# Second norm's rows of a hybrid decoder layer: transposed by VectorE blocks and DRAM, or by TensorE

## Chip, core and metric

The kernel runs on one core of a Trainium2 chip. The metric is the device time of one execution in microseconds; lower is better. Before the change three runs took 954.28, 956.22 and 958.12 us, median 956.22. PE is TensorE, DVE VectorE, ACT ScalarE, POOL GpSimd, and SP is the engine whose queue issues most DMAs.

## The reference

One decoder layer on 1024 tokens and 16 learned meta tokens of width 1024, in float32. The part that matters here is its second half:

```python
mix = jnp.concatenate([attn, rec], axis=-1) @ w_out[l]
h = h + rmsnorm(mix, g_post_mix[l])
u = rmsnorm(h, g_pre_ffn[l])
f = jnp.square(jax.nn.relu(u @ w_ff1[l])) @ w_ff2[l]
h = h + rmsnorm(f, g_post_ffn[l])
```

`rmsnorm(x, g)` multiplies each row by `rsqrt(mean(x*x) + 1e-6)` and by `g`. `mix` has 1024 columns, `w_ff1` is 1024 x 4096.

## The kernel before

Every product of float32 operands is made from three matmuls on a high and a low part of each operand (`mm3`, L125, L130, L131); `split` makes the parts, the high one on ScalarE (L96), the low one on VectorE (L99).

The output projection works on eight tiles of 128 tokens. `out_mm(t, ...)` fills two PSUM banks of 512 columns with `mix` for tile t: for t from 0 to 3 most of it beforehand, for t from 4 to 7 all 48 matmuls in the loop over t. `out_norm(t, ...)` then loads the rows of x (L939, on SP), squares the banks on ScalarE (L944), raises the mean to the power -0.5 on GpSimd (`rstd_of`, L170 to L176), scales the banks on VectorE (L950), adds x (L953), stores the sum h to the output (L954, on SP; the last stage reads or accumulates on it), squares h on ScalarE (L956), and multiplies h by its own scale on VectorE (L958). The result is u without its weight g_pre_ffn, with tokens in partitions.

The next product needs u with its 1024 columns in partitions. `u2_tiles(t, xn)` does this: eight TensorE transposes of 128x128 into PSUM (L970), evicted with the multiplication by g_pre_ffn as a column per partition, four on ScalarE (L981), two double ones on VectorE (L975). They land in `u2f[half]`, four buffers of 128x2x512 for the tokens 0 to 511 (half 0) and four for 512 to 1023 (half 1). In the loop over t, tiles 0 and 1 are transposed at t = 4, tiles 2 and 3 at t = 5, tile 4 at t = 6, tiles 5 and 6 at t = 7, and tile 7 after the loop.

The product with `w_ff1` is a scheme of seven block products for a 2x2 split (Strassen's kind). Four products of the first blocks (`p1`, `p2` for p = 0 and 1, 12 matmuls each) and two more `p1` need half 0 alone (`b11`, `b21` are its splits). Then `t_sums` adds and subtracts both halves (L996), the sums are split into `ot2`, and the long loop over sixteen column blocks begins (`prep_a` loads and combines the weights, L993 and L996; `product`). `p2` adds its result on VectorE (L1110).

The order of instructions on each engine is made by a scheduler when the program is built, and each engine executes its own in that order. SP's queue is one such row: a DMA that waits holds up all DMAs behind it. Buffers come from tagged rings: "d" has four buffers (x rows among others), "raw" two (h and raw weights), "ws" five, "c" eight.

Of the kernel before, what the change touches and what calls it, by code (L numbers as in the profile page):

```python
# [9 lines left out]
F32 = mybir.dt.float32  # L10
F32R = mybir.dt.float32r
AF = mybir.ActivationFunctionType
ALU = mybir.AluOpType
# [3 lines left out]
P = 128  # L17
D = 1024
KC = D // P
# [18 lines left out]
def hybrid_layer(  # L38
# [6 lines left out]
    nc = tc.nc  # L45
# [7 lines left out]
    dpool = ctx.enter_context(tc.tile_pool(name="dpool", bufs=1, space=DRAM))  # L53
# [4 lines left out]
    def slot(tag, shape, dt=F32):  # L58
        uid[0] += 1
        return slab.tile(shape, dt, tag=tag, name=f"{tag}{uid[0]}", bufs=bufs[tag])  # L60

    def pair(tag, shape):
        return slot(tag, shape, F32R), slot(tag, shape, F32R)
# [255 lines left out]
    def normed(b):  # L319
        if b == 0:  # L320
            return [
                (norm_rows(meta_t[:NMETA], NMETA), NMETA),
                (norm_first(xt[0], True), P), (norm_first(xt[1], False), P),
            ]
        rows = [(xt[2 * b], P), (xt[2 * b + 1], P)]
        return [(norm_rows(s[:m], m), m) for s, m in rows]
# [65 lines left out]
    xn = normed(0)  # L392
# [105 lines left out]
    for b in range(4):  # L498
# [3 lines left out]
        if b == 0:  # L502

            acc = [bank("acc"), bank("acc")]
# [3 lines left out]
            xn = [(norm_rows(xt[2], P, True), P)]  # L508
# [7 lines left out]
            for w, (t0, n), sink, tag in (  # L516
                (wq, (16, 256), sink_q0, "o"), (wx, piece, sink_x0, "acc"),
            ):
                acc = bank(tag)
# [10 lines left out]
    for h in range(2):  # L530
        r, o, m = HALF[h], HALF[1 - h], slice(P - NMETA, 2 * P)
# [62 lines left out]
    for b in range(2):  # L594
        pv = bank("pt", (P, 4, P))
        for i in range(4):
            o = NMETA + (4 * b + i) * P
# [288 lines left out]
    for cs in ((0, 1), (2, 3)):  # L886
# [13 lines left out]
        for c in cs:  # L900
            for half in range(2):
                y = ys[c][:, 512 * half : 512 * half + 512]
# [14 lines left out]
    t4_dram = dpool.tile([P, 2, 4, 512], F32, name="t4_dram")  # L917

    u2f = [[None] * 4 for _ in range(2)]

    def out_mm(t, po, kcs):
        half, o = t // 4, (t % 4) * P
# [8 lines left out]
                )  # L931

    def out_banks(t):
        tag = ("pt", "o", "acc", "s", "pt", "acc", "s", "pt")[t]
        return [bank(tag), bank(tag)]

    def out_norm(t, po):
        xr = slot("d", [P, D])
        nc.sync.dma_start(xr, x[t * P : (t + 1) * P, :])  # L939
        h = slot("raw", [P, D])  # L940
        ssq = [small.tile([P, 1], F32, name=f"sq{n}", tag=f"sq{n}") for n in range(2)]
        for n in range(2):
            c = slice(512 * n, 512 * n + 512)
            nc.scalar.activation(  # L944
                h[:, c], po[n], AF.Square, scale=RMS_SC, accum_out=ssq[n]
            )
        rs = rstd_of(ssq)
        for n in range(2):
            c = slice(512 * n, 512 * n + 512)
            nc.vector.scalar_tensor_tensor(  # L950
                h[:, c], po[n], rs, gmix_b[:, c], op0=ALU.mult, op1=ALU.mult
            )
        nc.vector.tensor_tensor(h, h, xr, op=ALU.add)  # L953
        nc.sync.dma_start(out[t * P : (t + 1) * P, :], h)  # L954
        ssq2 = small.tile([P, 1], F32, name="ssq", tag="ssq")
        nc.scalar.activation(xr, h, AF.Square, scale=RMS_SC, accum_out=ssq2)  # L956
        rs2 = rstd_of([ssq2])
        nc.vector.tensor_scalar(xr, h, rs2, None, op0=ALU.mult)  # L958
        return xr

    def u2_tiles(t, xn):
        half = t // 4
        if u2f[half][0] is None:
            u2f[half] = [slot("c", [P, 2, 512]) for _ in range(4)]
        o = (t % 4) * P
        for k4 in range(0, KC, 4):
            pt = bank("o", (P, 4, P))
            for i in range(4):
                kc = k4 + i
                nc.tensor.transpose(pt[:, i, :], xn[:, kc * P : (kc + 1) * P], ident)  # L970
            for i in range(0, 4, 2):
                kc = k4 + i
                dst = u2f[half][kc // 2]
                if k4:
                    nc.vector.tensor_tensor(  # L975
                        dst[:, :, o : o + P], pt[:, i : i + 2, :],
                        g_ffn_col[:, kc : kc + 2].to_broadcast([P, 2, P]), op=ALU.mult,
                    )
                    continue
                for n in range(2):  # L980
                    nc.scalar.activation(  # L981
                        dst[:, n, o : o + P], pt[:, i + n, :], AF.Copy,
                        scale=g_ffn_col[:, kc + n : kc + n + 1],
                    )
# [113 lines left out]
    xns = {}  # L1098
# [13 lines left out]
    for t in range(8):  # L1112
        po = pos[t] if t < 4 else out_banks(t)
        out_mm(t, po, range(6 if t < 4 else 0, KC))
        for t_ in {4: (0,), 5: (2,), 6: (4,), 7: (5,)}.get(t, ()):
            u2_tiles(t_, xns[t_])
        xns[t] = out_norm(t, po)
        for t_ in {4: (1,), 5: (3,), 7: (6,)}.get(t, ()):
            u2_tiles(t_, xns[t_])
        if t == 4:  # L1120
            a11_early.update(early(0, 0, pair("a", ESH)))
        if t == 5:
            b11 = operand(u2f[0][0:2])
            a12_early.update(early(1, 0, pair("ws", ESH)))
        if t == 6:
            b21 = operand(u2f[0][2:4])
            hl = slot("b", ESH, F32R), slot("e", ESH, F32R)
            a11_early.update(early(0, 2, hl))
# [380 lines left out]
```

## Time and profile before

| | us |
|---|---|
| median of three runs | 956.22 (954.28 to 958.12) |
| span of the profiled execution | 955.3 |
| PE busy in the span | 943.8 (99%) |
| DVE busy | 655.7 (69%) |
| ACT busy | 505.9 (53%) |
| POOL busy | 129.1 (14%) |

For the profiled execution the profile lists its span alone. A row of a timeline has start, duration, engine, line, operation, output and inputs, and in brackets the idle time before it with what ended it. In the chain of waits each row is a piece of the chain that ended last: start, length, and what ran. A row of windows lists, for a stretch of time, the busy time of PE, PEld (weight loads), DVE, ACT and POOL with their counts, then the TensorE clock that was granted, the DMA engines' busy share and GB/s. Matmuls overlap, so the distance between two starts is what one costs, not its length.

### The profile page before, as it was taken

Reading aid. Unit: us, or ns where it says so; the run is one execution under the profiler, and the core shown is the slowest. Engines: PE = TensorE matmul, PEld = TensorE weight load, DVE = VectorE, ACT = ScalarE, POOL = GpSimd, SP = SyncE. Lnnn points to the kernel's source line nnn. Section 1 sums busy time; section 2 is a strip of 40 time slices with the busy share of each in tenths; the row PEclk is TensorE's granted clock in tenths of the full one; section 3 lists DMA queues with packets and bytes.
Section 4 is the critical chain, followed back from the end, with each engine's and each line's share of the span. In section 5 each row is a group of like instructions: output and inputs, shape, how many; then the busy total and the mean of one; then the engine's idle time right before and its main releaser. Section 6 shows DMA issues by size and latency. Waiting matters only on the chain.

```text
span 955.3 us, 12432 instructions
## 1 busy us (share of the span) xinstructions
PE 943.8 (99%) x4728; PEld 789.7 (83%) x4728; DVE 655.7 (69%) x845; ACT 505.9 (53%) x854; POOL 129.1 (14%) x189
## 2 busy tenths in 40 slices
PE   9999999999999999999999999999999999999996
PEld 8999999877888878888888888888887788888885
DVE  6567987788856787665644465476667576779893
ACT  7537766568645554444655575654433343446441
POOL 4102563520021100010000000001121100001201
PEclk9999999999999999999999999999999999999999
DMA  8221010204226368674422364334777765647934
GB/s 271 56 67 23 24 45 24 67 23 131 83 109 185 133 220 264 198 253 144 155 89 88 111 203 127 104 113 114 175 180 186 185 199 177 192 139 196 246 65 89
DMA packets 88199, 130.21 MB, mean 136 GB/s; under 512 B 13702, under 2 KB 52630, under 8 KB 88140
## 3 DMA queue, kind: packets, MB, share of 16 engines
q1 hardware_dynamic: 78972, 104.44, 34.0%
q0 software_dynamic: 8880, 24.19, 12.2%
q8 instruction: 37, 0.61, 0.3%
q10 hardware_dynamic: 288, 0.79, 0.2%
q14 instruction: 22, 0.18, 0.1%
HBM read 109.93 MB, written 18.87 MB: 135 GB/s over the span
## 4 chain that ended last, share of the span: by engine, by line
PE 88%; DVE 5%; ACT 3%; DMA 2%; POOL 1%; issue 1%; SPq 0%; DVEq 0%; ACTq 0%; POOLq 0%
PE ps_acc L130 10%; PE ps_acc L131 10%; PE ps_acc L125 10%; PE ps_s L131 6%; PE ps_s L130 6%; PE ps_s L125 6%; PE ps_pt L130 6%; PE ps_pt L131 6%; PE ps_pt L125 6%; PE ps_o L130 5%; PE ps_o L131 5%; PE ps_o L125 5%; ACT c L82 1%; PE ps_o L691 1%; PE ps_acc L282 1%
## 5 line engine op out<-in xcount | busy, mean ns | idle before, releaser
L99 DVE TENSOR_TENSOR ws<-raw,ws 128x1024 fp32r<-128x1024 f32 (+1 forms) x69 | 82.6, 1197 | 76.1 <-ACT ws L96 24.3
L96 ACT CAST ws<-raw 128x1024 fp32r<-128x1024 f32 (+1 forms) x68 | 69.7, 1026 | 87.9 <-PE ps_o L130 23.9
L96 ACT CAST ws<-e 128x1024 fp32r<-128x1024 f32 x41 | 43.0, 1049 | 82.8 <-PE ps_o L130 35.3
L125 PE MATMUL ps_acc<-a,ws 128*128 128x256 f32 (+2 forms) x256 | 85.8, 335 | 0.0
L130 PE MATMUL ps_acc<-a,ws 128*128 128x256 f32 (+2 forms) x256 | 85.5, 334 | 0.0
L131 PE MATMUL ps_acc<-a,ws 128*128 128x256 f32 (+2 forms) x256 | 85.0, 333 | 0.0
L99 DVE TENSOR_TENSOR b<-b,b 128x1024 fp32r<-128x1024 f32 (+2 forms) x50 | 58.9, 1177 | 24.8 <-PE ps_o L130 19.1
L96 ACT CAST b<-b 128x1024 fp32r<-128x1024 f32 (+2 forms) x49 | 49.9, 1019 | 46.4 <-DVE b L996 41.0
L99 DVE TENSOR_TENSOR ws<-e,ws 128x1024 fp32r<-128x1024 f32 x41 | 50.1, 1223 | 32.4 <-ACT ws L96 18.9
L680 POOL TENSOR_SCALAR_AFFINE_SELECT c<-c 128x512 fp32r<-128x512 f32 x64 | 53.6, 858 | 67.6 <-ACT c L96 59.3
L125 PEld LDWEIGHTS ps_acc<-a,ws 128*128 128x128 f32 x256 | 48.3, 189 | 4.7 <-issue 0.2
L131 PEld LDWEIGHTS ps_acc<-a,ws 128*128 128x128 f32 x256 | 48.3, 189 | 4.5
L130 PEld LDWEIGHTS ps_acc<-a,ws 128*128 128x128 f32 x256 | 48.2, 188 | 4.4 <-issue 0.4
L125 PE MATMUL ps_acc<-ws,b 128*128 128x512 f32 (+1 forms) x120 | 46.3, 387 | 1.1 <-ACT ws L96 1.1
L130 PE MATMUL ps_acc<-ws,b 128*128 128x512 f32 (+1 forms) x120 | 46.3, 386 | 0.5 <-DVE ws L99 0.4
L131 PE MATMUL ps_acc<-ws,b 128*128 128x512 f32 (+1 forms) x120 | 46.1, 385 | 0.0
L125 PE MATMUL ps_pt<-ws,b 128*128 128x512 f32 x112 | 44.4, 396 | 0.0
L130 PE MATMUL ps_pt<-ws,b 128*128 128x512 f32 x112 | 44.1, 394 | 0.0
L131 PE MATMUL ps_pt<-ws,b 128*128 128x512 f32 x112 | 44.0, 393 | 0.0
L125 PE MATMUL ps_s<-ws,b 128*128 128x512 f32 x110 | 43.4, 395 | 0.0
L131 PE MATMUL ps_s<-ws,b 128*128 128x512 f32 x110 | 43.3, 394 | 0.0
L130 PE MATMUL ps_s<-ws,b 128*128 128x512 f32 x110 | 43.3, 393 | 0.0
(416 smaller groups left out, 2662.0 us busy)
## 6 DMA issues: line engine op xcount, KB each, us to landing
raw<-in_w_ff_dram SPq DMA_DIRECT2D x61, 512.0 KB, 4.1
e<-in_w_ff_dram SPq DMA_DIRECT2D x45, 512.0 KB, 4.0
a<-in_w_ff_dram SPq DMA_DIRECT2D x12, 512.0 KB, 6.6
s_dram<-a POOLq DMA_DIRECT2D x12, 512.0 KB, 3.7
c<-in_x_dram SPq DMA_DIRECT2D x8, 512.0 KB, 4.0
raw<-in_w_in_dram SPq DMA_DIRECT2D x8, 512.0 KB, 3.7
d<-in_x_dram SPq DMA_DIRECT2D x8, 512.0 KB, 3.3
out_dram<-raw SPq DMA_DIRECT2D x8, 512.0 KB
```

The lines of the kernel that those rows point to most:

```text
L82: ins = nc.scalar.activation(*args, **kwargs).ins
L96: nc.scalar.copy(hi, src)
L99: low = nc.vector.tensor_tensor(lo, src, f32(hi), op=ALU.subtract).ins
L125: ins = nc.tensor.matmul(dst, lh, rh, start=start, stop=False, skip_group_check=True).ins
L130: nc.tensor.matmul(dst, lh, rl, start=False, stop=False, skip_group_check=True)
L131: last_mm[0] = nc.tensor.matmul(dst, ll, rh, start=False, stop=stop, skip_group_check=True).ins.name
L282: last_mm[0] = nc.tensor.matmul(acc[:, :n], w[k // 2][:, kc, :], u[kc][k % 2][:, t0 : t0 + n], start=k == 0 and kc == 0, stop=k == last an ...
L680: nc.gpsimd.affine_select(out=p_[:, :, s], in_=f32(p_[:, :, 0]), pattern=[[0, 4], [g, P]], compare_op=op, fill=0.0, base=0, channel_multip ...
L691: nc.tensor.matmul(po[:, oc : oc + n], v, p_[:, pc : pc + n], start=first and k == 0, stop=last and k == 1, skip_group_check=True,)
```

## The change

For tiles 0 to 6 the TensorE transposes and their evictions go. The weight g_pre_ffn is loaded as a row for all partitions (`gpre_b`, by a DMA on ScalarE's queue, into a "ws" buffer), and VectorE multiplies h by its scale and by this row at once. `by_blocks` then turns the tile: one VectorE instruction transposes all 32x32 blocks into a second "d" buffer, and four DMAs, one for each 32 partitions, write it to a DRAM scratch of 512 KB a tile in runs of 1 KB. `u2_read`, called one tile later, fetches the eight 128x128 pieces from there into the same `u2f` buffers, each in one DMA of 512 runs of 128 B. All twelve DMAs are on SP's queue. Tile 7 keeps the old way, and its projection takes the banks "o" instead of "pt".

```diff
@@ -917,6 +917,10 @@
     t4_dram = dpool.tile([P, 2, 4, 512], F32, name="t4_dram")
 
     u2f = [[None] * 4 for _ in range(2)]
+    LAST_BY_DMA = 6
+    u2_dram = dpool.tile([LAST_BY_DMA + 1, 4, P, 2 * P], F32, name="u2_dram")
+    gpre_b = slot("ws", [P, D])
+    nc.scalar.dma_start(gpre_b, g_pre_ffn[0].partition_broadcast(P))
 
     def out_mm(t, po, kcs):
         half, o = t // 4, (t % 4) * P
@@ -931,7 +935,7 @@
                 )
 
     def out_banks(t):
-        tag = ("pt", "o", "acc", "s", "pt", "acc", "s", "pt")[t]
+        tag = ("pt", "o", "acc", "s", "pt", "acc", "s", "o")[t]
         return [bank(tag), bank(tag)]
 
     def out_norm(t, po):
@@ -955,8 +959,33 @@
         ssq2 = small.tile([P, 1], F32, name="ssq", tag="ssq")
         nc.scalar.activation(xr, h, AF.Square, scale=RMS_SC, accum_out=ssq2)
         rs2 = rstd_of([ssq2])
-        nc.vector.tensor_scalar(xr, h, rs2, None, op0=ALU.mult)
-        return xr
+        if t > LAST_BY_DMA:
+            nc.vector.tensor_scalar(xr, h, rs2, None, op0=ALU.mult)
+            return xr
+        nc.vector.scalar_tensor_tensor(
+            xr, h, rs2, gpre_b, op0=ALU.mult, op1=ALU.mult
+        )
+        return by_blocks(xr, u2_dram[t])
+
+    def by_blocks(xn, dram, tag="d"):
+        y = slot(tag, [P, 4, KC, 32])
+        nc.vector.transpose(y, xn.rearrange("p (k b d) -> p b k d", k=KC, b=4))
+        for a in range(4):
+            nc.sync.dma_start(
+                dram[a].rearrange("(b d) r -> d b r", b=4),
+                y[32 * a : 32 * a + 32].rearrange("p b k t -> p b (k t)"),
+            )
+        return dram
+
+    def u2_read(t, dram):
+        half, o = t // 4, (t % 4) * P
+        if u2f[half][0] is None:
+            u2f[half] = [slot("c", [P, 2, 512]) for _ in range(4)]
+        for kc in range(KC):
+            nc.sync.dma_start(
+                u2f[half][kc // 2][:, kc % 2, o : o + P].rearrange("p (a t) -> p a t", a=4),
+                dram[:, :, 32 * kc : 32 * kc + 32].rearrange("a p t -> p a t"),
+            )
 
     def u2_tiles(t, xn):
         half = t // 4
@@ -1112,11 +1141,9 @@
     for t in range(8):
         po = pos[t] if t < 4 else out_banks(t)
         out_mm(t, po, range(6 if t < 4 else 0, KC))
-        for t_ in {4: (0,), 5: (2,), 6: (4,), 7: (5,)}.get(t, ()):
-            u2_tiles(t_, xns[t_])
         xns[t] = out_norm(t, po)
-        for t_ in {4: (1,), 5: (3,), 7: (6,)}.get(t, ()):
-            u2_tiles(t_, xns[t_])
+        if t:
+            u2_read(t - 1, xns[t - 1])
         if t == 4:
             a11_early.update(early(0, 0, pair("a", ESH)))
         if t == 5:
```

## The prediction

> **What bounds the kernel now.** I read the page first (span, engine totals), then the chain of waits around the stage that the change touches, then the windows and timelines of that stage.
>
> ```profile
> span 955.3 us, 12432 instructions
> ...
> PE 943.8 (99%) x4728; PEld 789.7 (83%) x4728; DVE 655.7 (69%) x845; ACT 505.9 (53%) x854; POOL 129.1 (14%) x189
> ```
>
> TensorE is busy for 99% of the span, so whatever leaves its queue should leave the time, unless a wait takes its place. The chain shows how near such a wait is (start us, us, what):
>
> ```profile
> 325.58 0.99 POOL rs L176
> ...
> 326.59 0.26 DVE d L958
> ...
> 330.68 0.60 DVE d L1110
> ...
> 334.82 0.66 DVE c L975 x2
> ...
> 349.89 0.60 DVE d L996
> ...
> 351.15 0.50 PE ps_acc L131
> ```
>
> ```profile
> 326.00:337.00 11.00, 11.00 (x58) 9.16 (x56) 10.54 (x18) 7.62 (x15) 1.20 (x2) 1.00 0.50 146
> 337.00:348.00 11.00, 11.00 (x49) 8.98 (x48) 10.20 (x17) 6.13 (x11) 0.00 (x0) 1.00 0.71 239
> ```
>
> The chain leaves TensorE for the scale of the last token tile (rs, ready at 326.57), runs for 24.6 us through VectorE, and releases TensorE at 351.15. VectorE (fourth figure of a window) is busy 10.54 and 10.20 of 11 us there. TensorE lost next to nothing yet, but there is no slack: if rs of tile 7 comes later, or if TensorE gets there sooner, TensorE waits.
>
> **What leaves TensorE.** Tile 4's 48 matmuls run from the first to the second of these starts, and the chain gives eight transposes 0.87 us:
>
> ```profile
> 270.89 0.40 PE L125 MATMUL ps_pt<-ws,b 128*128 128x512 f32 x1
> 281.96 1.03 PE L970 MATMUL ps_o<-ident,d 128*128 128x128 f32 x8
> ```
> ```profile
> 282.12 0.87 PE ps_o L970 x8
> ```
>
> A matmul costs 11.07/48 = 0.231 us. Seven tiles' transposes are 7 x 0.87 = 6.1 us. That is the whole possible gain. Their evictions on ScalarE and VectorE go too; of those only the pair of tile 6 (0.66, row above) lay on the chain.
>
> **What comes in, per tile.** One VectorE block transpose of 128x1024, a multiplication by two operands for a cheaper one by a scalar, four 128 KB writes and eight 64 KB reads on SP's queue. Rows:
>
> ```profile
> 226.95 2.31 DVE L851 TENSOR_TENSOR_SCAN c<-b,c 128x1040 f32<-128x1040 f32 x1
> 229.19 1.20 DVE L99 TENSOR_TENSOR a<-raw,a 128x1024 fp32r<-128x1024 f32 x1
> 265.83 1.23 DVE L953 TENSOR_TENSOR raw<-raw,d 128x1024 f32<-128x1024 f32 x1
> 269.25 0.76 DVE L958 TENSOR_SCALAR d<-raw,rs 128x1024 f32<-128x1024 f32 x1 [2.12 <-POOL rs L176]
> 270.07 1.41 DVE L950 SCALAR_TENSOR_TENSOR raw<-ps_o,rs,e 128x512 f32<-128x512 f32 x2
> ```
> ```profile
> L208 SPq DMA_DIRECT2D raw<-in_w_in_dram x13: 368/368/817, 23.0 to 170.8; - x13
> ```
> ```profile
> L939 SPq DMA_DIRECT2D d<-in_x_dram x8: 328/337/454, 237.8 to 303.7; - x8
> ...
> DMA to landing us min/median/max: 3.3/3.3/3.3
> ```
> ```profile
> 186.37 0.59 SPq L867 DMA_DIRECT2D raw<-in_w_out_dram  x1
> ```
> ```profile
> 267.08 0.35 SPq L954 DMA_DIRECT2D out_dram<-raw  x1
> ```
> ```profile
> 270.38 0.60 ACT L944 ACTIVATE raw<-ps_acc 128x512 f32<-128x512 f32 x1 [2.13 <-DMA out_dram<-raw]
> ```
> ```profile
> e<-in_w_in_dram SPq DMA_DIRECT2D x2, 256.0 KB, 5.0
> ...
> ws<-ws POOLq DMA_DIRECT2D x2, 36.0 KB, 2.0
> ```
>
> - Transpose: not in this trace. Between 0.76 (one input, a scalar) and 2.31 (the scan); I take 1.2, the usual pass over such a tile. The multiplication: 1.2, like L953.
> - Writes: issue 0.35 to 0.59 (32 of 128 rows; L867 has 64 and takes 0.59), I take 0.45. Landing 2.0 (the 36 KB copy) to 3.3 (the 512 KB store issued at 267.08 released ScalarE at 270.38); I take 2.5. So 3 x 0.45 + 2.5 = 3.85.
> - Reads: 0.37 each to issue (L208, also many short runs; up to 0.59), 8 x 0.37 = 3.0.
> - Load of x: 3.3 alone, up to 5.0 (slowest 256 KB load above).
>
> The reads are 4096 runs of 128 B a tile. The nearest rows are two loads of w_q at 81 us (2 x 1024 runs of 256 B) and one of 1024 runs of 512 B at 121 us; the last two figures are DMA share and GB/s:
>
> ```profile
> 82.00:83.00 1.00, 1.00 (x11) 1.00 (x10) 0.84 (x3) 0.98 (x5) 0.00 (x0) 1.00 0.70 162
> 83.00:84.00 1.00, 1.00 (x11) 1.00 (x10) 0.97 (x3) 0.90 (x3) 0.31 (x1) 1.00 1.26 285
> 84.00:85.00 1.00, 1.00 (x11) 1.00 (x11) 1.00 (x3) 0.00 (x0) 0.42 (x2) 1.00 0.43 94
> ...
> 122.00:123.00 1.00, 1.00 (x11) 1.00 (x10) 1.00 (x2) 0.08 (x1) 0.82 (x4) 1.00 0.42 104
> 123.00:124.00 1.00, 1.00 (x11) 1.00 (x10) 0.97 (x3) 0.00 (x0) 1.00 (x3) 1.00 1.12 339
> 124.00:125.00 1.00, 1.00 (x11) 1.00 (x10) 0.97 (x3) 0.86 (x3) 1.00 (x2) 1.00 0.27 81
> ```
>
> A 256 B run costs 2.39 x 16 / 2048 = 18.7 ns of an engine, a 512 B run 1.81 x 16 / 1024 = 28.3 ns; a line through both gives 14 ns at 128 B. I take 16: 256 runs per engine are 4.1 us a tile, 1.1 us more than the reads' issue. The x row behind them comes late by half of that, I take 3.9.
>
> **The new wait.** SP's queue is now one chain. In the built order x of tile t+2 stands behind the reads of tile t, these behind the writes of tile t and the store of tile t+1; before, x rows were fetched ahead (first L939 at 237.8). The queue holds up x, and x holds up the sum that all later rows of the tile need. From the sum of tile t (L953's add, ended at 267.06 for tile 0) to that of tile t+2:
>
> - squares, GpSimd's power, until the multiplication: 267.06 to 269.25 = 2.2
> - multiplication 1.2, the next tile's two evictions 1.41, block transpose 1.2 = 3.8
> - writes 3.85, reads 3.0, x 3.9, add 1.2
>
> Together 17.95, so 9.0 a tile. TensorE needs 11.07 a tile, but it started far ahead. Sums: tile 2 at 285.0, tile 4 at 303.0. From there to tile 6 VectorE's own queue decides: two multiplications, two transposes, two pairs of evictions, two adds (10.0), six splits of 1.2 for the weights and the first half (7.2), 2.2 waiting for tile 4's scale and about 1.6 for tile 3's reads: 21.0, so 324.0. Tile 7: writes of tile 5 landed at about 325.2, reads 3.0, x 3.9, add 1.2: 333.4. Its scale is ready 2.2 later, at 335.6 instead of 326.6: 9.0 late.
>
> Behind it VectorE has nearly the same 24.6 us as before: the L975 pair of tile 6 (0.66) and two L1110 (1.2) are gone from it, one L996 (0.6) has moved into it: -1.3. TensorE is thus released 9.0 - 1.3 = 7.7 us late, and the 6.1 us it saved are spent waiting. The products of the first half cannot cover more: with tiles 4 to 7 done at 270.89 + 44.3 = 315.2, their six products of 12 matmuls end at 331.8.
>
> Two small terms. The load of g_pre_ffn is issued by ScalarE between activations of the earlier gate stage, whose chain ends in TensorE:
>
> ```profile
> L916 ACTq DMA_DIRECT2D e<-in_g_post_mix_dram x1: 380/380/380, 177.2 to 177.2; - x1
> ```
> ```profile
> 219.26 1.28 ACT L82
> ...
> 232.62 1.13 DVE a L99
> ...
> 233.79 0.50 PE ps_pt L130
> ```
>
> That is +0.4. And at the kernel's start TensorE was slow after rest: 11 of the 512-column matmuls of L308 in 4 us, where 17 would go:
>
> ```profile
> 1.50:3.50 2.00, 1.99 (x5) 1.60 (x6) 1.00 0.73 174
> 3.50:5.50 2.00, 2.00 (x6) 1.54 (x5) 1.00 0.94 347
> ```
>
> Six matmuls are 1.4 us. Whether a rest of several us in mid-kernel does the same no row shows: 0 to 1.4, I take 0.7. The Trainium skill (TensorE: Matmul & The Clock Gate, Rules for kernel authors) says that a gap of over about 3 us drops the clock to half until TensorE has been busy again for a window; by it the term would be the full 1.4, and +0.7 on the sum.
>
> Sum: 7.7 + 0.4 + 0.7 = +8.8, so 955.3 becomes 964.1. The profiled span lies 0.9 under the runs' median of 956.22; on the runs' scale I forecast 965.0.
>
> Bounds: low ends (transpose 0.76, writes 3.05, x 3.3) give a loop of 16.1, yet tile 7's add stands in VectorE's order behind the two L1110 adds, which need TensorE's fourth product, done at 315.2 + 11.1 = 326.3: then 0.6 + 1.2 + 2.2 = 330.3, so 3.7 - 1.3 = +2.4. High ends (transpose 2.31, writes 5.1, reads 4.7, x 5.0) give a loop of 23.1 and rs at about 351: +24.
>
> **Rivals.**
> 1. Faster: the transposes' 6.1 us come out. It needs rs of tile 7 by about 321.8 (326.6 + 1.3 - 6.1), or VectorE's row behind it to shrink by as much. For it: TensorE is at 99%, the DMA engines were 0.50 and 0.71 busy in the two windows above, and TensorE's own pace per tile is slower than the loop. Against: the floor of 330.3, which no quick DMA lifts. 955.3 - 6.1 = 949.2; 950 on the runs' scale. Chance 0.11.
> 2. The transfers land at their low ends: +2.4 + 0.4 = 958.1, 959 in runs, within 0.5%. For it: L939 landed in 3.3 each time. Against: here each x row follows 4096 small packets. Chance 0.15.
> 3. DMA engines set the pace: a 128 B run costs as much as a 512 B one, 28.3 ns, 7.2 us a tile instead of 4.1. 3.1 more in each of two loops, for tiles 5/6, for tile 7 and for the last read, 15.5 in all: 955.3 + 24.3 = 979.6, 980.5 in runs. For it: the runs are the shortest of the kernel. Against: 256 B was still a third cheaper than 512 B. The Trainium skill (DMA: Bandwidth & Descriptors, Specifications) puts the line rate at 512 B and up, and read-modify-write below; the trace shows 285 GB/s at 256 B against 339 at 512 B, a slope and no cliff there. Chance 0.12.
>
> **Chances and range.** My case (SP chain late, VectorE's row behind it) 0.62: own range 961 to 977. About 0.5% (4.8 us) is what a measurement of this kernel tells from no change. Faster 0.11, same 0.15, slower 0.74. Range 955 to 983: rival 1 and the far end of rival 3 are left out.
>
> **What would show it.** 56 fewer transposes; idle TensorE between about 332 and 346, released by VectorE; rs of tile 7 near 336; sums of tiles 9 us apart; waits of SP on u2_dram writes and of VectorE on x rows. A transpose far from 1.2, reads issued slower than 0.37, or x later than 3.9 shift it as given. Wrong if TensorE shows no gap there, or if most of the loss lies elsewhere.

## The result, and the profile after

The change made the kernel slower by two and a half per cent, more than twice what the prediction had. Median of five runs each, from the same chip:

| | before | after |
|---|---|---|
| median, us | 956.13 (954.28 to 958.12) | 980.31 (978.51 to 985.67) |
| ratio | | 1.026 [1.023, 1.029] |
| span of the profiled execution, us | 955.3 | 983.9 |
| DMA packets under 512 B | 13702 | 43734 |

The profiled execution of the kernel after is the slowest of its five (985.67); some 4 us of it are one more wait of TensorE far behind the changed stage (the 3.1 for ws in the list of waits below, at 784 us, with slow matmuls after it). The other 24 are in the stage, and they are read here.

From the page of the kernel after, its span, TensorE's line and the granted clock:

```profile
span 983.9 us, 12415 instructions
...
PE 946.6 (96%) x4672; PEld 789.0 (80%) x4672; DVE 662.8 (67%) x838; ACT 498.1 (51%) x826; POOL 127.9 (13%) x189
...
PEclk9999999999999959999999999999999999999999
```

The 56 transposes are gone (4672 matmuls, before 4728), but TensorE is busy for 96% of a longer span, and one slice of 25 us has half the clock. What it waited for (us in total, times, longest):

```profile
PE ps_o L999 <- DVE d L963: 8.2, 1, 8.2
PE ps_acc L125 <- ACT b L96: 7.2, 1, 7.2
PE ps_acc L125 <- ACT ws L96: 3.1, 1, 3.1
PE ps_pt L125 <- ACT a L96: 3.0, 1, 3.0
PE ps_acc L125 <- DVE raw L954: 2.0, 1, 2.0
PE ps_s L125 <- ACT b L96: 1.7, 1, 1.7
...
PE ps_pt L125 <- ACT ws L96: 1.5, 1, 1.5
```

The first row is the wait that stands where one was forecast: the transposes of tile 7 (L999) come behind its scaled rows (L963, L958 in the kernel before). The others stand around it: an eviction of tile 5 and two weight operands before, the first operands of the second half behind. The starts of all matmuls of 512 columns from 255 to 420 us, each less the 0.231 us that it may lie behind the one before it (and less the normal time of the transposes between), leave some 30.7 us, in the kernel before next to nothing. The three long breaks are 8.3 + 8.3 + 3.5 of it, the three short ones 2.2 + 1.6 + 1.9, and 4.8 are matmuls that ran slowly behind a break. 30.7 less the 6.1 of the transposes is 24.6: the whole change of the median.

VectorE's rows show when each sum came (L957, L953 before) and when tile 7's scale was used:

```profile
285.35 1.23 DVE L957 TENSOR_TENSOR raw<-raw,d 128x1024 f32<-128x1024 f32 x1 [5.53 <-DMA d<-in_x_dram]
...
296.59 1.23 DVE L957 TENSOR_TENSOR raw<-raw,d 128x1024 f32<-128x1024 f32 x1 [4.08 <-DMA d<-in_x_dram]
...
307.62 1.23 DVE L957 TENSOR_TENSOR raw<-raw,d 128x1024 f32<-128x1024 f32 x1 [3.87 <-DMA d<-in_x_dram]
...
332.31 1.23 DVE L957 TENSOR_TENSOR raw<-raw,d 128x1024 f32<-128x1024 f32 x1 [1.99 <-DMA d<-in_x_dram]
...
344.22 1.23 DVE L957 TENSOR_TENSOR raw<-raw,d 128x1024 f32<-128x1024 f32 x1 [3.02 <-DMA d<-in_x_dram]
...
347.66 0.75 DVE L963 TENSOR_SCALAR d<-raw,rs 128x1024 f32<-128x1024 f32 x1 [2.22 <-POOL rs L176]
```

These are tiles 2, 3, 4, 6 and 7. Each waits for its x row, as foreseen, but they come 11.2 us apart and not 9.0, and L963 starts at 347.66, where L958 started at 326.59: 21.1 us late, and not 9.0. One turn of SP's queue shows where a tile's time goes (start us, us of issue):

```profile
291.78 0.50 SPq L943 DMA_DIRECT2D d<-in_x_dram  x1
292.54 1.85 SPq L974 DMA_DIRECT2D u_dram<-d  x4
297.84 0.36 SPq L958 DMA_DIRECT2D out_dram<-raw  x1
298.39 4.61 SPq L985 DMA_DIRECT2D c<-u_dram  x8
303.04 0.50 SPq L943 DMA_DIRECT2D d<-in_x_dram  x1
303.64 0.93 SPq L1022 DMA_DIRECT2D raw<-in_w_ff_dram  x2
```

Read it as a loop of one tile: x of tile 3 is issued at 291.78 and its sum starts at 296.59 (4.8); the add takes 1.2; the store of that sum, which stands next in the queue, is issued at 297.84 and takes its turn (0.55); then the eight reads of tile 2 (4.65), and only then x of tile 4, at 303.04. 4.8 + 1.25 + 0.55 + 4.65 = 11.25. The weights' load for the products (L1022), which the kernel before issued at 287.93, stands behind all of that and comes at 303.64.

### The profile page after: what moved, and what is told of

It reads as the page before. It is cut to its first block, busy times and chain, and to the rows that moved or that the text cites. A ratio compares the mean times of both kernels' runs of the same rounds, so it can differ in the third digit from the quotient of the medians.

```text
span 983.9 us, 12415 instructions
## 1 busy us (share of the span) xinstructions
PE 946.6 (96%) x4672; PEld 789.0 (80%) x4672; DVE 662.8 (67%) x838; ACT 498.1 (51%) x826; POOL 127.9 (13%) x189
## 2 busy tenths in 40 slices
DMA packets 121943, 138.07 MB, mean 140 GB/s; under 512 B 43734, under 2 KB 86246, under 8 KB 121884
## 4 chain that ended last, share of the span: by engine, by line
PE 81%; DMA 6%; DVE 5%; ACT 3%; SPq 2%; issue 1%; POOL 1%; DVEq 0%; ACTq 0%; POOLq 0%
PE ps_acc L130 10%; PE ps_acc L125 9%; PE ps_acc L131 9%; PE ps_s L130 6%; PE ps_s L125 6%; PE ps_s L131 6%; PE ps_pt L125 5%; PE ps_pt L130 5%; PE ps_pt L131 5%; PE ps_o L125 5%; PE ps_o L130 5%; PE ps_o L131 5%; DMA raw<-in_w_ff_dram 2%; SPq L985 1%; ACT c L82 1%
## 5 line engine op out<-in xcount | busy, mean ns | idle before, releaser
L99 DVE TENSOR_TENSOR ws<-raw,ws 128x1024 fp32r<-128x1024 f32 (+1 forms) x69 | 82.7, 1199 | 76.8 <-ACT ws L96 27.4
L96 ACT CAST ws<-raw 128x1024 fp32r<-128x1024 f32 (+1 forms) x68 | 69.7, 1026 | 97.8 <-PE ps_o L130 24.1
L96 ACT CAST ws<-e 128x1024 fp32r<-128x1024 f32 x41 | 43.0, 1050 | 84.9 <-PE ps_o L130 27.2
L96 ACT CAST b<-b 128x1024 fp32r<-128x1024 f32 (+2 forms) x49 | 50.0, 1019 | 41.5 <-DVE b L1025 36.1
L125 PE MATMUL ps_pt<-ws,b 128*128 128x512 f32 x110 | 43.7, 397 | 0.0
L130 PE MATMUL ps_pt<-ws,b 128*128 128x512 f32 x110 | 43.3, 394 | 0.0
L131 PE MATMUL ps_pt<-ws,b 128*128 128x512 f32 x110 | 43.3, 393 | 0.0
```

What stands on the lines that cost most here:

```text
L96: nc.scalar.copy(hi, src)
L99: low = nc.vector.tensor_tensor(lo, src, f32(hi), op=ALU.subtract).ins
L125: ins = nc.tensor.matmul(dst, lh, rh, start=start, stop=False, skip_group_check=True).ins
L130: nc.tensor.matmul(dst, lh, rl, start=False, stop=False, skip_group_check=True)
L131: last_mm[0] = nc.tensor.matmul(dst, ll, rh, start=False, stop=stop, skip_group_check=True).ins.name
```

## The experiments

Each is the kernel after with one edit, or with several that were tried singly before; three to five rounds against the kernel before. "Scale" is when VectorE's row of tile 7 with its scale (L963) starts in the profiled execution of that run, and how much later than the 326.59 of before; "loss" is the median less that of the kernel before in the same comparison. e1, e10, e12, e15, e17 and e18 leave out the right order of the transposed rows: the second half computes on permuted values, with the same work on the engines.

| run | median, us | ratio | loss | scale |
|---|---|---|---|---|
| after | 980.31 | 1.026 [1.023, 1.029] | 24.2 | 347.66, +21.1 |
| e1 reads of 512 B runs | 974.53 | 1.020 [1.017, 1.023] | 19.2 | 342.83, +16.2 |
| e2 x on ScalarE | 975.78 | 1.020 [1.017, 1.023] | 20.4 | 344.45, +17.9 |
| e3 own buffers, tiles 0-3 | 973.22 | 1.017 [1.014, 1.021] | 17.9 | 342.69, +16.1 |
| e4 reads on ScalarE | 978.60 | 1.024 [1.020, 1.028] | 23.2 | 346.64, +20.1 |
| e5 four tiles | 970.86 | 1.016 [1.015, 1.018] | 15.7 | 343.69, +17.1 |
| e6 four tiles, own buffers | 965.35 | 1.010 [1.009, 1.012] | 10.2 | 334.70, +8.1 |
| e7 e3, stores on ScalarE | 975.19 | 1.021 [1.019, 1.022] | 20.0 | 346.27, +19.7 |
| e8 waits filled | 978.98 | 1.026 [1.023, 1.029] | 23.8 | 347.46, +20.9 |
| e9 x, stores on GpSimd | 980.70 | 1.026 [1.023, 1.029] | 25.2 | 349.24, +22.7 |
| e10 5 DMAs a tile | 970.28 | 1.014 [1.012, 1.017] | 14.7 | 339.67, +13.1 |
| e11 e6, x and stores on GpSimd | 965.32 | 1.010 [1.008, 1.013] | 9.8 | 335.98, +9.4 |
| e12 e3 + e9 + e10 | 966.49 | 1.011 [1.007, 1.014] | 11.0 | 338.72, +12.1 |
| e13 three tiles, own buffers | 960.59 | 1.004 [1.003, 1.006] | 4.8 | 329.98, +3.4 |
| e14 two tiles, own buffers | 955.67 | 1.000 [0.998, 1.001] | -0.1 | 324.51, -2.1 |
| e15 e6 with 5 DMAs a tile | 955.32 | 0.999 [0.998, 1.001] | -0.5 | 327.71, +1.1 |
| e16 one tile, own buffers | 956.08 | 1.000 [0.999, 1.001] | 0.3 | 325.25, -1.3 |
| e17 e6 with 512 B runs | 961.45 | 1.006 [1.004, 1.008] | 5.3 | 333.82, +7.2 |
| e18 e6 with one write a tile | 962.82 | 1.008 [1.006, 1.009] | 6.7 | 331.43, +4.8 |

The last two columns go together over the whole range: the loss is the lateness of tile 7's scale, within some 3 us. So the question for every run is what made that scale late.

**First round: one link of the loop at a time (e1 to e4).**

e1, the reads with runs of 512 B:

```diff
+        flat = dram.rearrange("a p (k t) -> (a p k t)", k=KC).rearrange(
+            "(k p t) -> k p t", k=KC, p=P
+        )
         for kc in range(KC):
-            nc.sync.dma_start(
-                u2f[half][kc // 2][:, kc % 2, o : o + P].rearrange("p (a t) -> p a t", a=4),
-                dram[:, :, 32 * kc : 32 * kc + 32].rearrange("a p t -> p a t"),
-            )
+            nc.sync.dma_start(u2f[half][kc // 2][:, kc % 2, o : o + P], flat[kc])
```

> Changed kernel with the same eight reads per tile (64 KB each), but each partition takes one run of 512 B instead of four of 128 B; the rows land in a wrong order, so the second half of the layer is computed on permuted values. T1, the row on SP's queue: an x row waits for the store of the tile before and for eight reads, 11.2 us a tile (x 4.7, add 1.2, store 0.5, reads 4.6), and a read costs SP its 0.51 us whatever its runs are. Then sums stay 10.3 to 11.2 us apart and the time is 974 to 982. T2, the DMA engines and their 128 B runs: the issue is held back by the engines and x arrives late behind the runs; with 512 B runs a read issues in 0.35 to 0.40, x lands in 3.3 to 3.8, sums are 8 to 9 us apart and the time is 960 to 968.

e2, and e4 in the same way for the reads (L985):

```diff
-        nc.sync.dma_start(xr, x[t * P : (t + 1) * P, :])
+        nc.scalar.dma_start(xr, x[t * P : (t + 1) * P, :])
```

> Changed kernel with the x rows of the second norm issued by ScalarE instead of SP, everything else alike. T1: x no longer stands behind the store and the reads, so the next add waits for the rest of the loop alone (scale, transpose, writes, reads, 8 to 9 us a tile or less): 960 to 970. T2: the x row's packets still queue on the same engines with the reads' runs, it lands 6 us or more after its issue, and the time stays at 973 to 982.

> Changed kernel with the reads of the turned rows issued by ScalarE, x rows, stores and writes stay with SP. T1: SP's row becomes x, writes, store, some 3 us a tile, but ScalarE now waits for the writes to land and gives 4 us a tile to the issues, between the squares that the scale needs: 962 to 974, sums 8 to 10 us apart. T2: 975 to 983, sums still 11 us apart.

e3, so that the x rows of tiles 2 to 4 needn't wait for a buffer:

```diff
-        return by_blocks(xr, u2_dram[t])
+        return by_blocks(xr, u2_dram[t], "c" if t < 4 else "d")
```

> Changed kernel with the turned rows of tiles 0 to 3 in buffers of the ring c instead of d, so that d holds four x rows again and they are fetched ahead as before the change. T1: sums of tiles 0 to 4 are 6 to 7.5 us apart (tile 4 by 295 instead of 308.8), tiles 5 to 7 still go one by one through the queue at 10 to 12 us; the scale of tile 7 comes 8 to 14 us sooner and the time is 964 to 972. T2: the reads take the engines' time in any case, sums are over 8 us apart, 973 or more.

By the loss, e1, e2 and e3 gained 4 to 6 us; the 1 us of e4 lies within the intervals. None gave what the removal of a single bound would have given. e2 and e4 missed the ranges of the first theory (T1) and lie in those of the second (T2). e1 lies at the lower end of T1's range, but its sums of tiles 2 to 4 came 8.6 and 10.9 us apart and a read held SP for 0.43, where T1 had 10.3 to 11.2 and 0.51: shorter issues alone shorten the loop. e3 has the time of T2 (973 or more) and the sums of T1: the first half runs at 7.1 us a tile (sums start at 279.57, 286.61, 293.85), yet tile 5's sum starts at 314.67, 21 us after tile 4's, and at 314.67 in e2 as well. Something else was close behind.

**Second round: what else stands in SP's queue (e5 to e8).**

e5 leaves tiles 4 to 7 to TensorE's transposes, in the order of the kernel before; e6 adds the edit of e3:

```diff
-    LAST_BY_DMA = 6
+    LAST_BY_DMA = 3
...
+        for t_ in {6: (4,), 7: (5,)}.get(t, ()):
+            u2_tiles(t_, xns[t_])
         xns[t] = out_norm(t, po)
-        if t:
+        if 0 < t < 5:
             u2_read(t - 1, xns[t - 1])
+        if t == 7:
+            u2_tiles(6, xns[6])
```

> Only tiles 0 to 3 go over DRAM; tiles 4 to 7 are transposed by TensorE, as in the kernel before, so 32 transposes leave TensorE (4 x 0.87 = 3.5 us) instead of 56. If the delay comes from the first four tiles' loop (x behind store and reads), the sum of tile 4 stays near 303 to 308 as in the changed kernel (307.6), tile 7's scale comes near 333, and the time is 960 to 968. If what costs is the loop of the second four tiles (their x, their stores and the row of reads, with no slack behind), the late first half is mostly caught up and the time is 953 to 959.

> As the run with tiles 0 to 3 alone, and the block transposes of these tiles go to buffers of their own class (c), so that their x rows are fetched ahead. With the same buffers for all seven tiles the first half ran at 7.1 us a tile and tile 4's sum began at 293.9 (before: 288.5). If the loop over x is the cost of the first half and the second half is as before, tile 7's scale comes within 3 us of the kernel before and TensorE keeps part of its 3.5 us: 950 to 957. If the 4096 small packets a tile also hold back the weights and stores of the second half, 957 to 965.

e5 lies above both of its ranges: tile 4's sum came at 307.28, as the first had it, but tile 7's scale at 343.69 and not near 333. e6 lies just above its second range, by which the small packets hold back what the second half needs. In e6 the x rows are no longer late, and tile 5 still is. ScalarE's and SP's rows of e6:

```profile
299.53 1.91 SPq L974 DMA_DIRECT2D u_dram<-c  x4
301.54 0.40 SPq L958 DMA_DIRECT2D out_dram<-raw  x1
```

```profile
305.43 0.60 ACT L948 ACTIVATE raw<-ps_acc 128x512 f32<-128x512 f32 x1 [8.55 <-DMA out_dram<-raw]
```

Tile 4's sum was done at 295.64 (it started at 294.46). Its store waited until 301.54 in the row behind eight reads and four writes, and tile 5's squares waited 8.55 us for the buffer that this store had to free. e7 takes the stores to ScalarE's queue, with all seven tiles and the buffers of e3:

```diff
-        nc.sync.dma_start(out[t * P : (t + 1) * P, :], h)
+        nc.scalar.dma_start(out[t * P : (t + 1) * P, :], h)
```

> All seven tiles over DRAM, first half's block transposes in buffers of class c (973.2 alone), and the stores of the sums issued by ScalarE instead of behind the reads on SP's queue. In the run with c alone tile 5's squares waited 9.2 us for a buffer that a store was still to free, and began at 305.5. If the store's place on SP's queue is the next link, tile 5's sum moves from 314.7 to 306 or earlier and the time to 964 to 970. If VectorE's order (five splits of 1.2 between tile 5's evictions and its sum, which wait for the reads of tile 3) is the next link, the sum stays within 2 us of 314.7 and the time at 971 to 975.

The sum of tile 5 didn't move (316.31), as the second of these said, and VectorE's rows of e7 bear out the reason that it gave:

```profile
305.14 1.41 DVE L954 SCALAR_TENSOR_TENSOR raw<-ps_acc,rs,e 128x512 f32<-128x512 f32 x2 [0.66 <-POOL rs L176]
308.62 1.23 DVE L99 TENSOR_TENSOR a<-raw,a 128x1024 fp32r<-128x1024 f32 x1 [2.07 <-ACT a L96]
...
315.17 1.23 DVE L99 TENSOR_TENSOR b<-c,b 128x1024 fp32r<-128x1024 f32 x1 [0.70 <-DMA c<-u_dram]
316.31 1.22 DVE L957 TENSOR_TENSOR raw<-raw,d 128x1024 f32<-128x1024 f32 x1
```

Tile 5's evictions came earlier than in e3 (305.14, there 307.59), but in VectorE's order five splits stand between them and the sum, and these waited for weights and for the reads of tile 3, both of which come through SP's row. So the order of VectorE hands the lateness of SP's row on to tile 5. Besides, the store itself came late once more, and held up ScalarE:

```profile
299.06 0.34 ACTq L958 DMA_DIRECT2D out_dram<-raw  x1
299.50 1.06 ACT L960 ACTIVATE d<-raw 128x1024 f32<-128x1024 f32 x1 [8.45 <-DMA c<-u_dram]
```

Its sum ended at 296.9 (start 295.72). What came last before it was a read (c<-u_dram) of an earlier tile. In the program as built, the DMAs of SP and ScalarE take eight semaphores in turn, and each waits for the DMA eight before it, on whichever of the two queues that is. So a store on the second queue still waited for a read on the first.

e8 prices the clock: TensorE gets 72 matmuls, whose bank nobody reads, to do in its two long waits.

```diff
     wa[0] = prep_a(0)
+    fill = bank("pt")
+    for _ in range(3):
+        product(fill, a11_early[2], b11, True)
     u2_tiles(7, xns[7])
+    for _ in range(3):
+        product(fill, a11_early[2], b11, True)
```

> The changed kernel with 72 more matmuls into a bank that nobody reads: 39 stand in TensorE's order ahead of the eight transposes of tile 7 (9.0 us of work at full clock, where it waits 8.2), 33 behind them (7.6 us where it waits 7.2). TensorE is busy through its two long waits. If the low granted clock after the waits (0.50 in 345 to 365 us) costs the time that the rows show (transposes 0.9 slower, some 12 matmuls 2.4 slower), the time falls by 2 to 3.5 us less the 0.5 that the filling overruns: 976.5 to 978.8. If the clock column is no cost of its own, the added work costs 0.5 to 2: 980.5 to 982.5.

The two windows, after and then e8 (busy us of PE, PEld, DVE, ACT, POOL, then granted clock, DMA share and GB/s):

```profile
345.00:365.00 20.00, 6.37 (x18) 4.69 (x19) 14.53 (x24) 9.47 (x17) 1.43 (x3) 0.50 0.86 248
```

```profile
345.00:365.00 20.00, 17.95 (x75) 14.02 (x74) 15.04 (x24) 9.53 (x17) 1.43 (x3) 0.92 0.86 255
```

The clock came back to 0.92, but the ratio to before is the same 1.026 and the median, between the two ranges, is only 1.3 us lower than after's, within the intervals. Other breaks of e8 (4.1 us at 330, and 1.7 behind the filling) were followed by slow matmuls in turn. So e8 does not settle the clock's share; it shows that the clock is not the main part.

**Third round: off the shared semaphores, and fewer DMAs (e9 to e12).** e9 issues x and the stores with nc.gpsimd.dma_start, whose DMAs have semaphores of their own. e10 writes each tile in one piece and reads it in four:

```diff
-        for a in range(4):
-            nc.sync.dma_start(
-                dram[a].rearrange("(b d) r -> d b r", b=4),
-                y[32 * a : 32 * a + 32].rearrange("p b k t -> p b (k t)"),
-            )
-        return dram
+        flat = dram.rearrange("a p r -> (a p r)").rearrange("(p f) -> p f", p=P)
+        nc.sync.dma_start(flat, y.rearrange("p b k t -> p (b k t)"))
+        return flat
...
-        for kc in range(KC):
+        for i in range(4):
             nc.sync.dma_start(
-                u2f[half][kc // 2][:, kc % 2, o : o + P].rearrange("p (a t) -> p a t", a=4),
-                dram[:, :, 32 * kc : 32 * kc + 32].rearrange("a p t -> p a t"),
+                u2f[half][i][:, :, o : o + P],
+                dram[:, 256 * i : 256 * i + 256].rearrange("p (k t) -> p k t", k=2),
             )
```

> The changed kernel, with the x rows and the stores of the sums issued by GpSimd: off SP's queue, and off the eight semaphores that SP's and ScalarE's DMAs share in turn (each of these DMAs waits for the one eight before it in program order, whichever of the two queues that is on). Theory now: a store or an x row on ScalarE gained little because it still waited for a read of an earlier tile on the shared semaphores (a store whose sum ended at 296.9 was issued at 299.06). If so, the loop loses the reads' issue and x's late start, 22.5 for two tiles becomes about 18 in the first half (sum of tile 4 near 300 instead of 307.6), tile 5's squares no longer wait for a buffer, and the time is 962 to 971. If moving them gains no more than ScalarE's queue did (975.8 and 975.2), the shared semaphores were not it: 973 to 979.

> The changed kernel with one write of 512 KB (runs of 4 KB) and four reads of 128 KB (runs of 512 B) a tile in place of four writes and eight reads: the same bytes in 5 DMAs instead of 12. The rows reach the products in a wrong order, so the output is not the reference's; the work on the engines is unchanged. Eight reads with runs of 512 B gave 974.5. If the number of DMAs in SP's row is the price (reads 4 x 0.5 instead of 8 x 0.55, writes 0.4 instead of 1.9, no turn of the eight semaphores to wait for), two tiles take 22.5 - 2.4 - 1.5 - 1 = 17.6 and the time is 958 to 967. If the landing times of the bytes are the price, it stays within 3 of the 974.5.

> Tiles 0 to 3 over DRAM with buffers of class c (965.3 so far), x rows and stores issued by GpSimd. In the run before, tile 4's sum ended at 295.6 but its store was issued at 301.5, behind reads and writes, and tile 5's squares waited 8.6 us for that buffer. If the store's place in SP's row was the cost, tile 5's squares begin near 299 instead of 305.4, tile 7's scale comes at 327 to 330 instead of 334.7, and the time is 954 to 960. If VectorE's longer order or the late first-half operand decides, it stays at 962 to 967.

> Seven tiles over DRAM with everything loosened at once: one write and four reads a tile (rows in a wrong order, output not the reference's), block transposes of the first half in buffers of class c, x rows and stores on GpSimd's queue. What is left is VectorE's order and the landing of one write and one read a tile. The prediction put the floor of this change at 2.4 us over before with 0.4 for the load of g_pre_ffn: 957 to 962 if VectorE's order is then the bound. If the second half's two-buffer loop (write landed, read, x) still binds, 963 to 970.

e9 is the instructive miss. The loop over x did become shorter, as expected (tile 4's sum starts at 300.07), and the time did not move. SP's and ScalarE's rows of e9:

```profile
292.08 2.59 SPq L974 DMA_DIRECT2D u_dram<-d  x4
300.47 4.90 SPq L985 DMA_DIRECT2D c<-u_dram  x8
305.53 0.93 SPq L1022 DMA_DIRECT2D raw<-in_w_ff_dram  x2
```

```profile
309.99 1.05 ACT L96 CAST a<-raw 128x1024 fp32r<-128x1024 f32 x1 [17.84 <-DMA raw<-in_w_ff_dram]
310.95 1.05 ACT L960 ACTIVATE d<-raw 128x1024 f32<-128x1024 f32 x1
```

and the waits of SP's queue in 285 to 312 us:

```profile
SPq L985 <- DMA u_dram<-d: 11.8, 5, 5.7
```

SP does nothing between 294.7 and 300.5 (the 5.7): at the head of its queue a read waits for the landing of a write. Behind it stands the weights' load, and ScalarE, which works in order, waits 17.84 us for these weights at a cast, with the squares of tile 4 (L960) behind the cast. Whatever is taken out of the row behind the reads, the next thing in it takes its place: x, then the stores, then the weights.

e10 took 10 us away, between its two ranges; e11 and e12 stayed in the upper ones, 10 and 11 us above before. In e12 tile 7's scale stands behind a step of VectorE that waited 4.6 us for weights, and SP's reads waited 21.2 us for writes between 290 and 345 us; what holds the rest there stays open. In e11 the DMA engines were fully taken (figure before the last); the second row is the same window of the kernel after:

```profile
290.00:300.00 10.00, 10.00 (x45) 8.15 (x44) 5.62 (x6) 1.15 (x2) 2.71 (x6) 1.00 1.00 269
```

```profile
290.00:300.00 10.00, 10.00 (x45) 8.17 (x44) 3.81 (x7) 2.42 (x6) 0.83 (x3) 1.00 0.77 193
```

**Fourth round: how many tiles, how many DMAs, how long the runs (e13 to e18).** e13, e14 and e16 are e6 with LAST_BY_DMA at 2, 1 and 0. e15 is e6 with the writes and reads of e10; e17 has the reads of e1 alone, e18 the one write alone.

> Tiles 0 to 2 over DRAM (block transposes in buffers of class c), tile 3 and tiles 4 to 7 by TensorE. With tiles 0 to 3 over DRAM (965.3) the transposes of tile 3 were done at 294.5, its four writes were issued at 299.5 behind the reads of tile 2, and its reads were all issued at 307.7; the first half's splits, tile 5's evictions and all that stands behind them in ScalarE's and VectorE's order waited for that. If this way of the last tile of the first half is the price, 953 to 957 (24 transposes leave TensorE, 2.6 us, and VectorE has about 1 us more a tile). If the price is VectorE's added work or the DMA load of the tiles before it, three quarters of the 9.9 us stay: 960 to 964.

> Tiles 0 and 1 alone over DRAM, with buffers of class c. Their rows are in place some 20 us before the first half's splits ask for them, so their way is hidden; TensorE has 16 transposes fewer (1.7 us). If only the last tiles' way counts: 953.5 to 955.5, at or just under the kernel before. If each tile over DRAM has its price by VectorE's work (1.2 for the transpose and 0.5 for the dearer multiplication, less 0.7 for its eviction): 956 to 959.

> Tile 0 alone over DRAM, 8 transposes fewer on TensorE (0.87 us). Whatever of the price comes with any use of the new way (the load of g_pre_ffn on ScalarE's queue, the instruction order that the added work brings) shows here: 954 to 956 if there is none, 957 or more if there is.

> Tiles 0 to 3 over DRAM with buffers of class c (965.3), one write and four reads with runs of 512 B a tile (rows in a wrong order, output not the reference's). With x ahead and the stores on GpSimd's queue the DMA engines were 0.91 and 1.00 busy in 280 to 300 us, against 0.77 in the changed kernel: they or SP's row are the second limit behind the loop over x. If so, a tile that takes 5 DMAs and 2.8 us of the DMA engines' time for its reads and writes, instead of 12 and about 6, brings tile 3's rows 5 us or more earlier and the time to 955 to 960. If the latency of one write and one read after it is the price whatever their size, 962 to 965.

> Tiles 0 to 3 over DRAM with buffers of class c, four writes and eight reads a tile as in the run with 965.3, but the reads in runs of 512 B instead of 128 B (rows in a wrong order, output not the reference's). One write and four reads of 512 B runs gave 955.3, 10 us less. If the short runs are what those 10 us were (the time of the DMA engines, the landing of the reads), most of it comes here too: 955 to 959. If it was the number of DMAs in SP's row: 961 to 965.

> Tiles 0 to 3 over DRAM with buffers of class c, the eight reads in runs of 128 B as in the run with 965.3, but one write of 512 KB a tile in place of four (rows in a wrong order, output not the reference's). SP's row loses three issues of 0.45 a tile and three turns of the eight semaphores. If the number of DMAs is the second limit: 961 to 963. If it is the short runs: 964 to 966.

One or two tiles change nothing that can be measured (the intervals are some 1.2 us to each side): what VectorE's transposes and the load of g_pre_ffn cost there is about what TensorE saves, 0.9 and 1.7 us, or less. The third costs 5 us, half of the four tiles' loss and not the three quarters of e13's second range, and the fourth 5 more. Nor do four tiles cost anything where they take 5 DMAs each with long runs (e15). There tile 3 is written when it is transposed, and tile 4's store follows within a microsecond:

```profile
294.16 0.45 SPq L974 DMA_DIRECT2D u_dram<-c  x1
...
295.18 0.80 SPq L958 DMA_DIRECT2D out_dram<-raw  x1
298.73 2.83 SPq L982 DMA_DIRECT2D c<-u_dram  x4
```

against 299.53, 301.54 and 304.42 in e6. Of the 10 us between e6 and e15, longer runs alone bring 4.9 (e17: loss 5.3 instead of 10.2) and one write alone 3.5 (e18: 6.7); the rest comes with four reads for eight, or with the two together. Both lie in the ranges that their expectations gave to the number of DMAs, but e17, which keeps the number, took away half of the 10 us. What goes together with the time is the length of SP's row, and both count and runs make it: the issue of tile 3's reads ended at 310.9 in e6, 309.2 in e18, 303.1 in e17 and 301.6 in e15. The load of the DMA engines as such is not it, for in e15 they were nearly full without a loss (the figure before the last):

```profile
290.00:300.00 10.00, 10.00 (x45) 8.13 (x44) 6.56 (x7) 2.81 (x6) 0.98 (x3) 1.00 0.98 320
```

e15 also bounds VectorE's added work: it has that work for four tiles, and its cost cannot be much over the 3.5 us that TensorE saves there.

No version beat the kernel before by more than the measurement tells: e15, whose rows are in the wrong order, and e14 are level with it.

## Why the prediction was wrong

Its sign and its place were right: TensorE waits for tile 7's scale behind SP's queue, where x rows stand behind reads (sums waiting for d<-in_x_dram, as it said). The size was wrong: 24.2 us for a forecast of 8.8. The step that failed is the loop over SP's queue, whose terms were too small; VectorE's row and the clock added the rest. Step by step:

- **What leaves TensorE**, 6.1 us: right, 56 matmuls fewer. **Block transpose and multiplication**, 1.2 each: right (L972 1.23, L965 1.28 us in the profile after). **g_pre_ffn**, +0.4: e16 has the same load, and no price can be told from zero.
- **The loop, 17.95 for two tiles.** This is the step that failed, in its terms. From tile 2 to tile 4 it was 307.62 - 285.35 = 22.3. Reads:

```profile
L985 SPq DMA_DIRECT2D c<-u_dram x56: 366/507/1672, 276.6 to 351.9; - x56
```

```profile
L974 SPq DMA_DIRECT2D u_dram<-d x28: 325/442/1207, 272.7 to 341.7; - x28
...
DMA to landing us min/median/max: 3.8/4.1/4.9
```

  They took 0.51 each to issue and 0.04 between them, 4.6 for eight in place of 3.0: the row L208 (0.37) was not the nearest after all. A write landed 4.1 after its issue, not 2.5, so the writes' term is 5.4 and not 3.85. x took 4.8, not 3.9. Together 1.6 + 1.6 + 0.9 = 4.1, and 17.95 + 4.1 = 22.05 is what the rows show. The issue time of 0.45 a write was right. With these terms a second loop, of one tile (x, add, store, reads), is as long: 11.25. The prediction had its parts, 3.9 + 1.2 + 0.35 + 3.0 = 8.5, under its 9.0, and didn't name it. SP's waits between 280 and 350 us, the three longest, show that this loop held the queue longer: 11.6 us at stores (L958) that waited for the sum, 4.5 at reads that waited for a write.

```profile
SPq L958 <- DVE ms L172: 6.6, 2, 3.4
SPq L958 <- DVE raw L957: 5.0, 3, 1.9
SPq L985 <- DMA u_dram<-d: 4.5, 5, 1.8
```

- **21.0 from tile 4 to tile 6, by VectorE's own queue**, and 9.4 to tile 7: 24.7 and 11.9 in the profile. Both sums still wait for x there; the weights' loads and the reads of tile 3, which the splits ask for, stand in the same row of SP. By here the scale is 12 us later than forecast (21.1 and not 9.0 behind): most of the 15.4 that the forecast fell short. Of the 12, 5.9 had come by the sum of tile 4 (ended at 308.85, forecast 303.0), 3.7 came from there to tile 6, and 2.5 to tile 7. The short breaks are part of the same lateness: the products of the first half ended at 339.9 and not at 331.8, since TensorE waited for tile 5's evictions and for weights on the way, and the long waits stood between 340 and 361, not at 332 to 346.
- **VectorE's row behind the scale, nearly as before (-1.3).** It became +1.2. Both kernels have the same matmuls behind the stage, so each can be set beside the one with as many behind it. The matmul at 361.39, where TensorE starts again, stood in the kernel before at

```profile
339.06 0.39 PE L130 MATMUL ps_pt<-b,a 128*128 128x512 f32 x1
```

  It is 22.3 late, and the scale 21.1. Two of the three long waits ended with casts of ScalarE, where VectorE had been forecast: the last one with a cast of weights (a L96), whose load was issued at 353.50, behind the reads of tile 6 in SP's row:

```profile
346.06 6.30 SPq L985 DMA_DIRECT2D c<-u_dram  x8
```

- **The slow clock, 0.7 (0 to 1.4).** Too small: some 2.3. From 361.39 on the matmuls run 0.43 us apart, and 0.23 again some 5 us later:

```profile
361.39 0.79 PE L125 MATMUL ps_pt<-b,a 128*128 128x512 f32 x1 [2.96 <-ACT a L96]
361.98 0.63 PE L130 MATMUL ps_pt<-b,a 128*128 128x512 f32 x1
362.41 0.63 PE L130 MATMUL ps_acc<-b,e 128*128 128x512 f32 x1
...
366.98 0.40 PE L131 MATMUL ps_pt<-b,a 128*128 128x512 f32 x1
367.21 0.40 PE L125 MATMUL ps_pt<-b,a 128*128 128x512 f32 x1
```

  Over these twelve the lateness grows from 22.3 to 24.7. The rest of the 4.8 us of slow matmuls lies before the long waits. So the loss in the profile is 21.1 + 1.2 + 2.3 = 24.6, where the forecast had 9.0 - 1.3 + 0.7, and 0.4 for g_pre_ffn.

  The Trainium skill (TensorE: Matmul & The Clock Gate, Part 1: The HAM clock gate) gives 427 ns between cold matmuls of 512 columns and half the clock until one busy window of about 3.4 us; this trace agrees in the rate, with 0.43, and in the clock, with a granted 0.50, while its slow stretch lasted some 5 us. The rule on gaps that the prediction cites stands, under the same title of the Trainium skill, in the section Why this matters for your kernels; here breaks under 3 us were followed by slow matmuls too (last section). Whether a filled wait would save the 2.3 e8 leaves open: ten slow matmuls followed its own break of 1.7 at the same place.
- **Floor of +2.4, by VectorE's order.** Not reached and not contradicted: with a short row the loss is nil for four tiles (e15), and still 11.0 for seven (e12).
- **Rival 1 (faster)**: TensorE's gain didn't come out even where the row was shortened (e12, e15). **Rival 2 (low-end landings)**: landings were at their high ends. **Rival 3 (DMA engines set the pace, 980.5)** has the right time and the wrong mechanism. By it the reads alone would take the engines 7.2 us a tile. In the trace the 10224 packets of 128 B that started from 280 to 312 us took 12.9 ns each on average, 256 x 12.9 = 3.3 us a tile, less than the 4.1 of the sum. In e11 the engines were full (1.00), in e15 nearly so (0.98) without a loss: a full share alone does not make the time.

The measured time lies inside the stated range of 955 to 983 and outside the 961 to 977 of the prediction's own case. The high end of the bounds (+24) took issue at 0.59, x at 5.0 and writes at 5.1, close to what came, but also a transpose of 2.31, which took 1.23: that the number is the same is partly luck. The middle was chosen from rows of transfers that ran alone; here fourteen a tile follow each other.

## What to carry to other kernels

Before a step is moved to DMA, write down the whole row of that queue for one turn of the loop: every issue, the wait at its head, and all that stands behind it, weights and stores included; if the row is longer than the pace at which tiles come (here over 7 us of issues a tile, where sums came 5.7 us apart before), each load behind it becomes late in turn, and taking one out only shows the next. A DMA that waits for another to land shouldn't stand at the head of a queue on which anything urgent follows. A round trip over DRAM was free here for tiles whose rows are needed late, the first two of eight, and for the first four where the row was short (5 DMAs a tile).

## What the runs showed of the hardware

- An issue of a 64 KB read with 128 B runs held SP for 0.51 us, with 512 B runs 0.43 (e1), a 512 KB write with 4 KB runs 0.34 (e10): the price follows the pattern more than the bytes. x, a plain row load, rose from a median of 0.34 to 0.50 when it followed such reads.
- The four writes of 32 rows landed after 2.2 to 2.3 us with two or four tiles and buffers of their own (e14, e6) and after 4.1 in the kernel after.
- A packet of 128 B took a DMA engine 12.9 ns in the kernel after, one of 512 B 27.4 and one of 1 KB 46.0 (280 to 312 us).
- Breaks of TensorE well under 3 us were followed by slow matmuls too, not each time: some ten of them behind one of 2.1 us in e6, none behind one of 2.2 in e1.
